# A dilated convolution on one core: start-up reordered, one-bank PSUM tiles, dummy matmuls ahead of the data

## The chip, the cores and the metric

The kernel runs on one core of one Trainium2 chip. The metric is device time in microseconds (us) of one execution; lower is better. Profiles come from single executions. The span of a profile (first to last instruction) is 1.8 us shorter than the time of the same execution (142.9 against 144.67 us for the kernel before).

Engines are named as in the profile: PE is TensorE's matmul side, PEld its weight loads, DVE is VectorE, ACT is ScalarE, POOL is GpSimd, SP is SyncE; PEq, SPq and ACTq are sequencers. L141 is line 141 of that kernel's file.

## The reference

A 3x3 convolution with dilation 2 over a batch of 16 images of 64 channels, 64x64 pixels, giving 128 channels, all float32:

```python
for kh in range(3):
    for kw in range(3):
        output[b, co] += weight[co, ci, kh, kw] * x_pad[b, ci, kh*2:kh*2+64, kw*2:kw*2+64]
```

## The kernel before

Two images share the 128 partitions (64 channels each), so each matmul uses 64 rows of the array, and the matmuls of the two images, one on each half of the rows, run together. Weights are transposed on PE with an identity; inputs arrive as float32 and are cast to float16 by DVE and ACT. A group is two tiles of 8 image rows (512 columns each); its nine taps (the nine places of the 3x3 window) accumulate in PSUM, the memory that matmuls write, and DVE and ACT evict it, that is, copy it to where it can be stored from. PSUM space for 512 float32 columns is called a bank here.

```python
# cut to the lines that the change touches
G = 2
# ...
cpool = ctx.enter_context(tc.tile_pool(name="cpsum", bufs=4, space=bass.MemoryType.PSUM))   # four tiles of two banks
# ...
nc.gpsimd.dma_start(out=w16, in_=weight.rearrange("o i h w -> o (i h w)"))   # casts in flight
wt_ps_a = cpool.tile([CO, G * NB], f32, tag="ps", name="wt_a")               # eight taps in one tile
for t, (dh, dw) in enumerate(taps):
    # ... two transposing matmuls, one per half of the partitions ...
    if t in (3, 7):
        nc.scalar.copy(out=w_sb[:, (t - 3) * CO : (t + 1) * CO], in_=wt_ps_a[...])
# ... then four input chunks per pair, of 18, 16, 16 and 14 rows, cast by DVE and ACT in turn ...
else:   # the last group of all, tile by tile, both tiles in the same ps
    for ti in range(G):
        for t in range(ntaps):
            for hb in range(2):
                conv_matmul(x3, ps, g, ti, t, hb, t == 0, t == ntaps - 1)
        # evict ps[0] half on DVE, ps[1] half on ACT, store both
```

The order of instructions on each engine is chosen by the scheduler, not by the program text.

## Time and profile before

144.34 us, median of 4 runs. The span can be cut at two events: the first convolution matmul, and the start of the last eviction, which is when the last matmul is through.

| part of the span | from | to | us |
|---|---|---|---|
| start | 0 | first convolution matmul, 11.70 | 11.7 |
| stream | 11.70 | last eviction starts, 136.93 | 125.2 |
| tail | 136.93 | end, 142.9 | 6.0 |

These are lines of the page of the kernel before: the span, the busy shares, and the rows of the 40-slice picture (each digit is the busy share of 3.6 us, in tenths).

```profile
span 142.9 us, 2675 instructions
PE 125.9 (88%) x1170; PEld 56.0 (39%) x1170; DVE 50.8 (36%) x49; ACT 50.4 (35%) x53; POOL 21.4 (15%) x49
...
PE   0029999999999999999999999999999999999730
PEclk9999999999999999999999999999999999999995
DMA  4999999999999999999999979393958667599791
```

PE is idle for most of three slices, then full. DVE and ACT have much room. DMA is full in the first half, but once the convolution runs PE never waits for it. This is the start in the timeline of the kernel before (columns: start, duration, engine, line, operation, output<-input, and in brackets the idle time before it and what ended it).

```profile
8.07 0.38 PE L86 MATMUL wt_a<-ident,w 128*64 128x128 f16 x1 [8.07 <-DMA w<-in_weight_dram]
...
9.56 0.94 ACT L122 CAST x_sb<-x 128x896 f16<-128x896 f32 x1 [2.12 <-DMA x<-in_x_dram]
10.41 0.58 ACT L89 CAST w_sb<-wt_a 128x512 f16<-128x512 f32 x1
...
11.04 0.27 PE L86 MATMUL wt_a<-ident,w 128*64 128x128 f16 x1 [2.12 <-ACT w_sb L89]
...
11.70 8.59 PE L141 MATMUL ps<-x_sb,w_sb 64*128 64x512 f16 x58
...
15.62 0.15 PEld L141 LDWEIGHTS <-w_sb 64*128 64x128 f16 x2 [0.28 <-issue]
16.05 0.15 PEld L141 LDWEIGHTS <-w_sb 64*128 64x128 f16 x2 [0.28 <-issue]
16.46 3.55 PEld L141 LDWEIGHTS <-w_sb 64*128 64x128 f16 x34 [0.27 <-issue]
```

Three things stand here. The weights arrive at 8.07 us. The first transposes are done by about 8.9, but ACT copies them only at 10.41, because its queue holds the cast of the fourth input chunk first and that chunk arrives at 9.56; PE waits 2.12 us for the copy. And from 11.70 to 16.46 us the weight loads come in pairs mostly 0.42 us apart (0.32 before the narrower matmuls of 384 columns at the image's edge), later without gaps: PE runs at half rate for 4.7 us. The PEclk row reads 9 there all the same: it takes the clock as full until the trace's first clock record (these records lie in the packed trace; `prof` shows only what is made of them). That first record, a stretch at full clock, begins at 16.44 us, just where the gaps end; so the half rate is the clock. The end of the same timeline shows one stall:

```profile
134.21 0.69 DVE L179 COPY o_sb<-ps 128x512 f32<-128x512 f32 x1 [0.72 <-PE ps L141]
...
134.95 1.96 PE L141 MATMUL ps<-x_sb,w_sb 64*128 64x512 f16 x18 [0.78 <-DVE o_sb L179]
...
136.93 0.69 DVE L179 COPY o_sb<-ps 128x512 f32<-128x512 f32 x1 [2.03 <-PE ps L141]
```

The last tile's matmuls wait 0.78 us until DVE has evicted the other half of the PSUM tile that they write. Their nine pairs then take 1.96 us, 0.22 us a pair: that is full rate.

### The profile page before, as it was taken

The numbers are of one execution on the slowest core, as the hardware profiler recorded it, in microseconds if no ns is written. First come the engines' busy times: TensorE is split into PE (matmuls) and PEld (weight loads), VectorE is DVE, ScalarE is ACT, GpSimd is POOL, SyncE is SP. The second block draws the span as 40 slices with busy tenths as digits, with TensorE's granted clock in tenths as the row PEclk, the third lists the DMA queues.
The fourth block names the chain that finished last, engine by engine and source line by source line (L and its number), as shares of the span: only waits on it lengthen the run. The fifth ranks groups of instructions, "written<-read, shape, count | busy, mean of one in ns | idle before, by whom it ended". The sixth has DMA issues, their size and how long they took to land.

```text
span 142.9 us, 2675 instructions
## 1 busy us (share of the span) xinstructions
PE 125.9 (88%) x1170; PEld 56.0 (39%) x1170; DVE 50.8 (36%) x49; ACT 50.4 (35%) x53; POOL 21.4 (15%) x49
## 2 busy tenths in 40 slices
PE   0029999999999999999999999999999999999730
PEld 0024344444444444444444444444444444444310
DVE  0213355443535352424253534433333322222510
ACT  3245374352254325241425244522222222222410
POOL 6000003020201102020202020202002020222410
PEclk9999999999999999999999999999999999999995
DMA  4999999999999999999999979393958667599791
GB/s 115 342 398 408 414 420 413 415 427 426 421 419 432 421 417 409 423 429 409 415 380 421 430 323 431 124 411 147 390 204 330 257 280 312 218 408 390 287 390 76
DMA packets 10108, 50.66 MB, mean 355 GB/s; under 512 B 1136, under 2 KB 1264, under 8 KB 6512
## 3 DMA queue, kind: packets, MB, share of 16 engines
q0 software_dynamic: 5200, 33.18, 56.2%
q1 hardware_dynamic: 4896, 17.30, 30.9%
q8 instruction: 9, 0.15, 0.4%
q14 instruction: 3, 0.02, 0.1%
HBM read 17.07 MB, written 33.55 MB: 354 GB/s over the span
## 4 chain that ended last, share of the span: by engine, by line
issue 59%; PE 18%; POOL 11%; DMA 5%; ACT 2%; SPq 1%; POOLq 1%
PE ps L141 18%; POOL out_dram L203 11%; DMA x<-in_x_dram 5%; SPq L113 1%; ACT o_sb L171 1%; ACT x_sb L122 1%; POOLq L237 0%; POOL out_dram L185 0%; ACT w_sb L89 0%; PE wt_a L87 0%; PE wt_a L86 0%; POOLq L203 0%; POOLq L185 0%
## 5 line engine op out<-in xcount | busy, mean ns | idle before, releaser
L141 PE MATMUL ps<-x_sb,w_sb 64*128 64x512 f16 (+1 forms) x1152 | 124.4, 375 | 0.8 <-DVE o_sb L179 0.8
L141 PEld LDWEIGHTS <-w_sb 64*128 64x128 f16 x1152 | 54.7, 94 | 70.2 <-issue 4.1
L170 DVE COPY o_sb<-ps 128x1024 f32<-128x1024 f32 x31 | 38.0, 1225 | 58.5 <-PE ps L141 58.5
L171 ACT COPY o_sb<-ps 128x1024 f32<-128x1024 f32 x31 | 31.4, 1013 | 65.6 <-PE ps L141 65.6
L203 POOL DMA_DIRECT2D out_dram<-o_sb x34 | 18.0, 534 | 113.3 <-ACT o_sb L171 112.8
L122 ACT CAST x_sb<-x 128x1024 f16<-128x1024 f32 (+1 forms) x16 | 15.9, 994 | 17.1 <-DMA x<-in_x_dram 10.2
L120 DVE CAST x_sb<-x 128x1152 f16<-128x1152 f32 (+1 forms) x16 | 11.6, 726 | 25.6 <-DMA x<-in_x_dram 15.4
L86 PE MATMUL wt_a<-ident,w 128*64 128x128 f16 x8 | 1.3, 322 | 10.2 <-DMA w<-in_weight_dram 8.1
L86 PEld LDWEIGHTS <-w 128*64 128x64 f16 x9 | 1.2, 207 | 8.1 <-DMA w<-in_weight_dram 8.1
L179 DVE COPY o_sb<-ps 128x512 f32<-128x512 f32 x2 | 1.4, 691 | 2.7 <-PE ps L141 2.7
L182 ACT COPY o_sb<-ps 128x512 f32<-128x512 f32 x2 | 1.2, 586 | 3.1 <-PE ps L141 3.1
L87 PEld LDWEIGHTS <-w 128*64 128x64 f16 x9 | 1.2, 207 | 2.2 <-issue 2.2
L122 ACT ACT_TABLE_LOAD x1 | 1.3, 1283 | 0.7 <-PEq L223 0.7
L185 POOL DMA_DIRECT2D out_dram<-o_sb x2 | 1.1, 547 | 2.7 <-DVE o_sb L179 2.7
L87 PE MATMUL wt_a<-ident,w 128*64 128x128 f16 x8 | 1.4, 335 | 0.0
L89 ACT CAST w_sb<-wt_a 128x512 f16<-128x512 f32 x2 | 1.2, 583 | 0.7 <-PE wt_a L87 0.7
L72 POOL DMA_DIRECT2D w<-in_weight_dram x1 | 0.7, 675 | 0.8 <-POOLq L223 0.8
L100 POOL MEMSET x_sb<- 128x128 f16 x3 | 0.7, 235 | 0.0
L101 POOL MEMSET x_sb<- 128x128 f16 x3 | 0.7, 234 | 0.0
L87 PE MATMUL wt_b<-ident,w 128*64 128x128 f16 x1 | 0.3, 323 | 0.0
L86 PE MATMUL wt_b<-ident,w 128*64 128x128 f16 x1 | 0.3, 322 | 0.0
masks.py:199 POOL TENSOR_SCALAR_AFFINE_SELECT ident<-ident 128x128 f16<-128x128 f16 x1 | 0.3, 308 | 0.0
(6 smaller groups left out, 0.9 us busy)
## 6 DMA issues: line engine op xcount, KB each, us to landing
out_dram<-o_sb POOLq DMA_DIRECT2D x28, 1024.0 KB, 8.5
x<-in_x_dram SPq DMA_DIRECT2D x16, 512.0 KB, 9.6
x<-in_x_dram SPq DMA_DIRECT2D x8, 576.0 KB, 7.2
x<-in_x_dram SPq DMA_DIRECT2D x8, 448.0 KB, 12.2
out_dram<-o_sb POOLq DMA_DIRECT2D x6, 512.0 KB, 4.5
out_dram<-o_sb SPq DMA_DIRECT2D x2, 256.0 KB, 3.1
out_dram<-o_sb POOLq DMA_DIRECT2D x2, 256.0 KB, 3.3
w<-in_weight_dram POOLq DMA_DIRECT2D x1, 144.0 KB, 6.8
```

Source lines behind the costliest of these rows:

```text
L86: nc.tensor.matmul(out=wt_ps[0:CI, c0 : c0 + CO], lhsT=w_slice, rhs=ident)
L87: nc.tensor.matmul(out=wt_ps[CI : 2 * CI, c0 : c0 + CO], lhsT=w_slice, rhs=ident)
L89: nc.scalar.copy(out=w_sb[:, (t - 3) * CO : (t + 1) * CO], in_=wt_ps_a[:, (t - 3) * CO : (t + 1) * CO],)
L113: nc.sync.dma_start(out=x32[:, lo:hi], in_=x_pair[pb, :, lo:hi])
L120: nc.vector.tensor_copy(out=x3[:, lo:hi, pad : pad + W], in_=x32[:, lo:hi, :])
L122: nc.scalar.copy(out=x3[:, lo:hi, pad : pad + W], in_=x32[:, lo:hi, :])
L141: nc.tensor.matmul(out=po, lhsT=lhsT, rhs=rhs, start=first, stop=last)
L170: nc.vector.tensor_copy(out=o_sb0[:, sl], in_=ps[0])
L171: nc.scalar.copy(out=o_sb1[:, sl], in_=ps[1])
L179: nc.vector.tensor_copy(out=o_sb0[:, e0:e1], in_=ps[0][:, ti * NB : (ti + 1) * NB])
L182: nc.scalar.copy(out=o_sb1[:, e0:e1], in_=ps[1][:, ti * NB : (ti + 1) * NB])
L203: nc.gpsimd.dma_start(out=out_img[2 * pb + bi, :, e0:e1], in_=o_sb[bi][:, e0:e1],)
```

## The change

It aims at all three places: weights earlier, copies not behind casts, clock released before the convolution, and PSUM tiles of one bank in eight buffers. The core of the diff, with lines shortened and left out:

```diff
-    chunk_rows = [(0, GR + d)]
+    chunk_rows0 = [(0, ROWS + d), (ROWS + d, CR + d)] + chunk_rows[1:]   # first pair: 10 + 8 rows
-    cpool = ... bufs=4 ...            # tiles of two banks
+    cpool = ... bufs=8 ...            # tiles of one bank
+    w32 = wpool.tile([CO, CI * KH * KW], f32, name="w32")
+    nc.scalar.dma_start(out=w32, in_=weight.rearrange("o i h w -> o (i h w)"))
-    nc.gpsimd.dma_start(out=w16, in_=weight.rearrange("o i h w -> o (i h w)"))
+    for _ in range(9):
+        nc.tensor.matmul(out=warm_ps, lhsT=warm_sb[:, :CO], rhs=warm_sb)
+    nc.vector.tensor_copy(out=w16, in_=w32)
+    ctx.enter_context(tc.manual_schedule(engines={DVE, Activation}))     # program order there
+    emit_cast(0, chunk_rows0[0][0], chunk_rows0[0][1], "v")
+    emit_cast(0, chunk_rows0[1][0], chunk_rows0[1][1], "s")
     for t, (dh, dw) in enumerate(taps):
+        wt_ps = cpool.tile([CO, NB], f32, tag="ps", name=f"wt{t}")       # one tile per tap
+        # transposes; copies by ACT and DVE in turn
+    # casts of the other three chunks only after the weight copies
-    for g in range(ngroups): ...      # two row tiles per PSUM tile, evicted as 128x1024
+    for ti in range(ntiles): ...      # one row tile per PSUM tile, evicted as 128x512
```

Stores keep their sizes, but all those of the last pair are now issued by POOL and SP side by side; before, only its last group's were.

More of the change, by code (lines that the diff above doesn't have):

```diff
@@ L39 @@
     assert H % ROWS == 0
-    G = 2
-    assert ntiles % G == 0
-    ngroups = ntiles // G
     NB = ROWS * W
-    GR = G * ROWS
-    chunk_rows = [(0, GR + d)]
-    for g in range(1, ngroups - 1):
-        chunk_rows.append((g * GR + d, (g + 1) * GR + d))
-    chunk_rows.append(((ngroups - 1) * GR + d, H))
-    nchunks = len(chunk_rows)
-    assert nchunks == ngroups
+    CR = 2 * ROWS
+    nchunks = ntiles // 2
+    chunk_rows = [(0, CR + d)]
+    for c in range(1, nchunks - 1):
+        chunk_rows.append((c * CR + d, (c + 1) * CR + d))
+    chunk_rows.append(((nchunks - 1) * CR + d, H))
+    assert nchunks == 4
+    chunk_rows0 = [(0, ROWS + d), (ROWS + d, CR + d)] + chunk_rows[1:]
     taps = [(0, 0)]
@@ L68 @@
     opool = ctx.enter_context(tc.tile_pool(name="opool", bufs=4))
-    cpool = ctx.enter_context(tc.tile_pool(name="cpsum", bufs=4, space=bass.MemoryType.PSUM))
+    cpool = ctx.enter_context(tc.tile_pool(name="cpsum", bufs=8, space=bass.MemoryType.PSUM))
+    w32 = wpool.tile([CO, CI * KH * KW], f32, name="w32")
+    nc.scalar.dma_start(out=w32, in_=weight.rearrange("o i h w -> o (i h w)"))
     w16 = wpool.tile([CO, CI * KH * KW], f16, name="w16")
-    nc.gpsimd.dma_start(out=w16, in_=weight.rearrange("o i h w -> o (i h w)"))
     ident = wpool.tile([P, P], f16, name="ident")
@@ L77 @@
     w_sb = wpool.tile([P, ntaps * CO], f16, name="w_sb")
-    wt_ps_a = cpool.tile([CO, G * NB], f32, tag="ps", name="wt_a")
-    wt_ps_b = cpool.tile([CO, G * NB], f32, tag="ps", name="wt_b")
-    for t, (dh, dw) in enumerate(taps):
-        kh = dh // d + KH // 2
-        kw = dw // d + KW // 2
-        w_slice = w16.rearrange("o (i k) -> o i k", k=KH * KW)[:, :, kh * KW + kw]
-        wt_ps, c0 = (wt_ps_a, t * CO) if t < 8 else (wt_ps_b, 0)
-        nc.tensor.matmul(out=wt_ps[0:CI, c0 : c0 + CO], lhsT=w_slice, rhs=ident)
-        nc.tensor.matmul(out=wt_ps[CI : 2 * CI, c0 : c0 + CO], lhsT=w_slice, rhs=ident)
-        if t in (3, 7):
-            nc.scalar.copy(
-                out=w_sb[:, (t - 3) * CO : (t + 1) * CO],
-                in_=wt_ps_a[:, (t - 3) * CO : (t + 1) * CO],
-            )
-        elif t == 8:
-            nc.scalar.copy(out=w_sb[:, t * CO : (t + 1) * CO], in_=wt_ps_b[:, :CO])
     x3_bufs = []
@@ L111, in emit_input_dma, with emit_cast @@
         x32_tiles[pb] = x32
-        for lo, hi in chunk_rows:
+        for lo, hi in (chunk_rows0 if pb == 0 else chunk_rows):
             nc.sync.dma_start(out=x32[:, lo:hi], in_=x_pair[pb, :, lo:hi])
-    def emit_cast(pb, ci_):
-        lo, hi = chunk_rows[ci_]
+    def emit_cast(pb, lo, hi, engine):
         x3 = x3_bufs[pb % NXB]
         x32 = x32_tiles[pb]
-        if ci_ % 2 == 0:
+        if engine == "v":
             nc.vector.tensor_copy(out=x3[:, lo:hi, pad : pad + W], in_=x32[:, lo:hi, :])
@@ L124, with conv_matmul @@
     emit_input_dma(0)
-    for ci_ in range(nchunks):
-        emit_cast(0, ci_)
-    def conv_matmul(x3, ps, g, ti, t, hb, first, last):
+    warm_sb = wpool.tile([P, NB], f16, name="warm_sb")
+    nc.vector.memset(warm_sb, 0.0)
+    warm_ps = cpool.tile([CO, NB], f32, tag="ps", name="warm_ps")
+    for _ in range(9):
+        nc.tensor.matmul(out=warm_ps, lhsT=warm_sb[:, :CO], rhs=warm_sb)
+    nc.vector.tensor_copy(out=w16, in_=w32)
+    ctx.enter_context(
+        tc.manual_schedule(engines={mybir.EngineType.DVE, mybir.EngineType.Activation})
+    )
+    emit_cast(0, chunk_rows0[0][0], chunk_rows0[0][1], "v")
+    emit_cast(0, chunk_rows0[1][0], chunk_rows0[1][1], "s")
+    for t, (dh, dw) in enumerate(taps):
+        kh = dh // d + KH // 2
+        kw = dw // d + KW // 2
+        w_slice = w16.rearrange("o (i k) -> o i k", k=KH * KW)[:, :, kh * KW + kw]
+        wt_ps = cpool.tile([CO, NB], f32, tag="ps", name=f"wt{t}")
+        nc.tensor.matmul(out=wt_ps[0:CI, 0:CO], lhsT=w_slice, rhs=ident)
+        nc.tensor.matmul(out=wt_ps[CI : 2 * CI, 0:CO], lhsT=w_slice, rhs=ident)
+        dst = w_sb[:, t * CO : (t + 1) * CO]
+        if t % 2 == 0:
+            nc.scalar.copy(out=dst, in_=wt_ps[:, 0:CO])
+        else:
+            nc.vector.tensor_copy(out=dst, in_=wt_ps[:, 0:CO])
+    emit_cast(0, chunk_rows[1][0], chunk_rows[1][1], "v")
+    emit_cast(0, chunk_rows[2][0], chunk_rows[2][1], "s")
+    emit_cast(0, chunk_rows[3][0], chunk_rows[3][1], "v")
+    def conv_matmul(x3, ps, ti, t, hb, first, last):
         dh, dw = taps[t]
-        tile_idx = g * G + ti
-        r0 = tile_idx * ROWS
+        r0 = ti * ROWS
         lo = max(r0, -dh)
@@ L139, in conv_matmul @@
         ]
-        po = ps[hb][:, ti * NB + (lo - r0) * W : ti * NB + (hi - r0) * W]
+        po = ps[hb][:, (lo - r0) * W : (hi - r0) * W]
         nc.tensor.matmul(out=po, lhsT=lhsT, rhs=rhs, start=first, stop=last)
@@ L146 @@
         o_sb1 = opool.tile([P, HW], f32, tag="osb")
-        o_sb = (o_sb0, o_sb1)
+        first_pair = pb == 0
         last_pair = pb == npairs - 1
-        flush_after = {ngroups // 2 - 1: (0, HW // 2), ngroups - 1: (HW // 2, HW)}
         if last_pair:
-            flush_after = {g: (g * G * NB, (g + 1) * G * NB) for g in range(ngroups)}
-        for g in range(ngroups):
+            flush_after = {
+                ti: ((ti - 1) * NB, (ti + 1) * NB) for ti in range(1, ntiles - 2, 2)
+            }
+            flush_after[ntiles - 2] = ((ntiles - 2) * NB, (ntiles - 1) * NB)
+            flush_after[ntiles - 1] = ((ntiles - 1) * NB, ntiles * NB)
+        else:
+            flush_after = {
+                ntiles // 2 - 1: (0, HW // 2),
+                ntiles - 1: (HW // 2, HW),
+            }
+        for ti in range(ntiles):
             ps = [
-                cpool.tile([CO, G * NB], f32, tag="ps", name=f"ps{hb}")
-                for hb in range(2)
-            ]
-            tail_group = last_pair and g == ngroups - 1
-            if not tail_group:
-                for t in range(ntaps):
-                    first = t == 0
-                    last = t == ntaps - 1
-                    for ti in range(G):
-                        for hb in range(2):
-                            conv_matmul(x3, ps, g, ti, t, hb, first, last)
-                sl = slice(g * G * NB, (g + 1) * G * NB)
+                cpool.tile([CO, NB], f32, tag="ps", name=f"ps{hb}") for hb in range(2)
+            ]
+            for t in range(ntaps):
+                for hb in range(2):
+                    conv_matmul(x3, ps, ti, t, hb, t == 0, t == ntaps - 1)
+            if pb + 1 < npairs:
+                if ti == 2:
+                    emit_input_dma(pb + 1)
+                elif ti == 4:
+                    emit_cast(pb + 1, chunk_rows[0][0], chunk_rows[0][1], "v")
+                    emit_cast(pb + 1, chunk_rows[1][0], chunk_rows[1][1], "s")
+                elif ti == 5:
+                    emit_cast(pb + 1, chunk_rows[2][0], chunk_rows[2][1], "v")
+                    emit_cast(pb + 1, chunk_rows[3][0], chunk_rows[3][1], "s")
+            sl = slice(ti * NB, (ti + 1) * NB)
+            if ti % 2 == 0:
                 nc.vector.tensor_copy(out=o_sb0[:, sl], in_=ps[0])
@@ L172 @@
             else:
-                for ti in range(G):
-                    for t in range(ntaps):
-                        for hb in range(2):
-                            conv_matmul(x3, ps, g, ti, t, hb, t == 0, t == ntaps - 1)
-                    e0 = (g * G + ti) * NB
-                    e1 = e0 + NB
-                    nc.vector.tensor_copy(
-                        out=o_sb0[:, e0:e1], in_=ps[0][:, ti * NB : (ti + 1) * NB]
-                    )
-                    nc.scalar.copy(
-                        out=o_sb1[:, e0:e1], in_=ps[1][:, ti * NB : (ti + 1) * NB]
-                    )
-                    nc.gpsimd.dma_start(out=out_img[2 * pb, :, e0:e1], in_=o_sb0[:, e0:e1])
+                nc.scalar.copy(out=o_sb0[:, sl], in_=ps[0])
+                nc.vector.tensor_copy(out=o_sb1[:, sl], in_=ps[1])
+            if ti in flush_after:
+                e0, e1 = flush_after[ti]
+                nc.gpsimd.dma_start(out=out_img[2 * pb, :, e0:e1], in_=o_sb0[:, e0:e1])
+                if last_pair:
                     nc.sync.dma_start(
@@ L188 @@
                     )
-            if pb + 1 < npairs:
-                if g == 1:
-                    emit_input_dma(pb + 1)
-                elif g == 2:
-                    emit_cast(pb + 1, 0)
-                    emit_cast(pb + 1, 1)
-                elif g == 3:
-                    emit_cast(pb + 1, 2)
-                    emit_cast(pb + 1, 3)
-            if not tail_group and g in flush_after:
-                e0, e1 = flush_after[g]
-                for bi in range(2):
+                else:
                     nc.gpsimd.dma_start(
-                        out=out_img[2 * pb + bi, :, e0:e1],
-                        in_=o_sb[bi][:, e0:e1],
+                        out=out_img[2 * pb + 1, :, e0:e1], in_=o_sb1[:, e0:e1]
                     )
```

## The prediction

> **What bounds it now.** TensorE in the middle, latency at both ends. The timeline shows the first convolution matmul at 11.70 us and the last one's evictions starting at 136.93 us of a 142.9 us span. Between them PE is busy without a break (the windows view reads 10.00 of 10 us in every middle stretch), except one 0.78 us stall at 134.2 us, where the waits view shows PE waiting for the DVE eviction of the tail group's half. VectorE and ScalarE are at 36% and 35%; DMA runs full, about 420 GB/s, in the first half, but PE never starves.
>
> So span = start (11.7) + stream (125.2) + tail (6.0). The stream holds avoidable time: weight loads of the convolution are spaced 0.42 us a pair from 11.7 to 16.4 us, then the tail's nine pairs take 1.96 us (0.22 each). About 4.7 us run at half rate, about 2.35 us lost. The Trainium skill, "TensorE: Matmul & The Clock Gate", Part 1, says the array starts at half clock and is released after a busy free-running window of about 3.4 us; this trace agrees in kind (release about 5.4 us after the dense start at 11.04). The page's PEclk row does not show it.
>
> **What the change does.**
> 1. Start. The weights land at 8.07 us now (issued at 1.25, 6.8 us to landing on the software queue, 144 KB packed), then transposes stall 2.1 us on a ScalarE copy that itself sat behind an input cast waiting for DMA. After: ScalarE's hardware queue, raw f32 (twice the destination bytes), issued about 0.75. The first input chunk of 576 KB landed 4.4 us after its issue; weights plus the new 10-row chunk are 608 KB, so I expect both at 5.0-5.5. Then the DVE cast of weights (estimate 0.43 us, from 0.69-0.76 for 1024-1152 columns), transposes (0.11 us a pair), ScalarE's 8-row cast (estimate 0.6, waiting for its chunk at about 6.0), the first weight copy (0.27), the ninth transpose waiting for a bank. Convolution starts at about 7.1 instead of 11.7: -4.6 us, all critical.
> 2. Nine dummy matmuls fill PE from about 1.1 to 5 us (0.43 each at half rate), so the clock should be released when the convolution starts: -2.35 us if so, about 0 if the burst straddles two windows. I give the release about 65%.
> 3. One-bank PSUM tiles in 8 buffers: the 0.78 us tail stall goes. Evictions are halved: DVE two of 0.69 for one of 1.23, ScalarE two of 0.59 for 1.01, some 5 us more busy time each, off the critical path.
> 4. Casts in program order: inputs are prefetched less far ahead, still about 15 us early. No PE gain or loss expected.
> 5. Matmuls and weight loads of the convolution: same number (1152); the tail after the last matmul stays about 6.0 us.
>
> **Sum.** 144.3 - 4.6 - 0.8 - (2.35 or 0) = 136.6 or 138.9; predicted 137.2 us, 8 in 10 within 135.8 to 139.8. Faster by over 2%: 0.94; within 2%: 0.05; slower: 0.01.
>
> **What would show it.** Timeline: weights' cast on DVE near 5.2-5.6, first convolution matmul near 7.1, weight loads spaced 0.21 us a pair from there (0.42 means the warm-up failed). Waits: no PE wait of note after the start; last matmul about 122 us after the first; 6.0 us after it. DMA row: less than full in the first half, fuller later.
>
> **What would make it wrong.** Weights delayed behind input packets (start at 8 or later); clock not released; ScalarE's in-order cast of the late chunk holding all weight copies; evictions held behind a cast that waits for input, stalling PE in mid-stream; output stores backing up at the end, lengthening the tail.

## The result, and the profile after

136.95 us median (136.78 to 139.25, 11 runs) against 144.44 us (143.44 to 145.03, 15 runs). The ratio is 0.949 (95% interval 0.947 to 0.952). Ratios here are the mean time of one kernel's fast runs over that of the other's fast runs of the same rounds, so they are not quite the ratio of the medians.

Ten of the 11 runs lie between 136.78 and 137.15 us. The eleventh, 139.25 us, is the one whose profile came first; the record classes it as slow, and the ratio leaves it out. So the unaltered kernel was run again (label after_again: 137.13 us median, 136.95 to 137.20, 6 runs), and its profile, of an execution of 137.12 us, is the one shown here. From its page:

```profile
span 135.2 us, 2764 instructions
PE 127.0 (94%) x1179; PEld 57.9 (43%) x1179; DVE 56.5 (42%) x87; ACT 53.7 (40%) x86; POOL 19.9 (15%) x45
...
PE   6799999999999999999999999999999999999910
PEclk9999999999999999999999999999999999999998
DMA  4999999999999999999999999999979294799790
```

Its timeline, start and end:

```profile
1.19 3.62 PE L110 MATMUL warm_ps<-warm_sb 128*128 128x512 f16 x9 [1.19 <-DVE warm_sb L107]
...
5.07 0.46 DVE L111 CAST w<-w 128x576 f16<-128x576 f32 x1 [3.93 <-DMA w<-in_weight_dram]
5.58 0.33 PE L122 MATMUL wt<-ident,w 128*64 128x128 f16 x1 [0.77 <-DVE w L111]
5.90 0.62 ACT L103 CAST x_sb<-x 128x512 f16<-128x512 f32 x1 [3.45 <-DMA x<-in_x_dram]
6.42 0.94 ACT L126 CAST w_sb<-wt 128x128 f16<-128x128 f32 x5
...
6.99 12.90 PEld L145 LDWEIGHTS <-w_sb 64*128 64x128 f16 x124
...
128.96 0.59 ACT L190 COPY o_sb<-ps 128x512 f32<-128x512 f32 x1 [1.16 <-PE ps L145]
```

Weights are in at 5.07 us, the copies follow their transposes (ACT's after its 8-row cast), the convolution starts at 7.00, its weight loads run without gaps from the first on, and the last eviction starts at 128.96. The waits view has no wait of PE for anything once the convolution has begun. From the chain of waits of the same profile (start, duration, what):

```profile
0.74 4.31 DMA w<-in_weight_dram
7.06 115.70 PE ps L145 x1093
```

Cut as above, with the profiled executions of the other runs for later use:

| profile | start | stream | tail | span |
|---|---|---|---|---|
| before | 11.70 | 125.23 | 5.97 | 142.9 |
| changed (after_again) | 7.00 | 121.96 | 6.24 | 135.2 |
| changed, the 139.25 us execution | 7.03 | 123.73 | 6.24 | 137.0 |
| no_warm | 7.21 | 123.23 | 6.26 | 136.7 |
| old_weight_load | 8.27 | 123.54 | 6.29 | 138.1 |
| unsplit_first | 7.98 | 123.65 | 6.27 | 137.9 |
| free_schedule | 9.90 | 123.91 | 6.19 | 140.0 |
| before_in_order | 10.45 | 124.46 | 5.99 | 140.9 |
| before_tail_banks | 11.58 | 123.33 | 6.89 | 141.8 |
| weights_first | 6.70 | 121.96 | 6.24 | 134.9 |
| split_tail | 6.92 | 121.99 | 6.39 | 135.3 |

So of the 7.7 us of span, the start gave 4.70, the stream 3.27, and the tail took back 0.27. Five profiles with full rate throughout have a stream of 121.96 to 121.99 us (the two not in the table are those of after_beside, 121.96, and of copies_first_split_tail, 121.98), whatever was done around it; that is the pace of PE.

The slow execution of the same kernel differs in one thing. These are its weight loads at the start:

```profile
7.02 0.13 PEld L145 LDWEIGHTS <-w_sb 64*128 64x128 f16 x4
...
9.67 0.15 PEld L145 LDWEIGHTS <-w_sb 64*128 64x128 f16 x2 [0.27 <-ACT x_sb L103]
10.09 0.15 PEld L145 LDWEIGHTS <-w_sb 64*128 64x128 f16 x2 [0.27 <-issue]
10.52 9.45 PEld L145 LDWEIGHTS <-w_sb 64*128 64x128 f16 x88 [0.27 <-issue]
```

The loads are 0.42 us apart until 10.52: 3.5 us at half rate. The dummy matmuls had run, but the clock had not been released: the trace's first clock record, at full clock, begins at 10.65 us, against 4.27 us in after_again, and the transposes before the convolution take 0.32 us here against 0.28 there. DMA is as busy in both (the slices after the first read 9), so it does not explain the half rate. Nor does only a slow run show it: no_warm below does.

### The profile page after: what moved, and what is told of

The parts are those of the page before. It is cut to its first block, busy times and chain, and to the rows that moved or that the text cites. A ratio compares the mean times of both kernels' runs of the same rounds, so it can differ in the third digit from the quotient of the medians.

```text
span 137.0 us, 2764 instructions
## 1 busy us (share of the span) xinstructions
PE 129.0 (94%) x1179; PEld 58.3 (43%) x1179; DVE 56.5 (41%) x87; ACT 54.0 (39%) x86; POOL 19.9 (14%) x45
## 2 busy tenths in 40 slices
DMA packets 10252, 50.80 MB, mean 371 GB/s; under 512 B 1152, under 2 KB 1152, under 8 KB 6656
## 4 chain that ended last, share of the span: by engine, by line
PE 87%; issue 4%; DMA 3%; POOL 1%; POOLq 0%; DVE 0%
PE ps L145 86%; DMA w<-in_weight_dram 3%; PE wt L122 1%; POOL out_dram L195 1%; POOLq L234 0%; DVE w L111 0%; PE wt L123 0%; POOLq L195 0%
## 5 line engine op out<-in xcount | busy, mean ns | idle before, releaser
L145 PEld LDWEIGHTS <-w_sb 64*128 64x128 f16 x1152 | 56.0, 94 | 67.5 <-issue 1.9
L191 DVE COPY o_sb<-ps 128x512 f32<-128x512 f32 x32 | 22.1, 692 | 35.3 <-PE ps L145 35.3
L187 DVE COPY o_sb<-ps 128x512 f32<-128x512 f32 x32 | 22.1, 692 | 33.0 <-PE ps L145 33.0
L188 ACT COPY o_sb<-ps 128x512 f32<-128x512 f32 x32 | 18.8, 587 | 36.8 <-PE ps L145 36.8
L190 ACT COPY o_sb<-ps 128x512 f32<-128x512 f32 x32 | 18.8, 587 | 35.1 <-PE ps L145 35.1
L103 ACT CAST x_sb<-x 128x1024 f16<-128x1024 f32 (+2 forms) x16 | 15.6, 977 | 4.3 <-DMA x<-in_x_dram 4.3
L101 DVE CAST x_sb<-x 128x1024 f16<-128x1024 f32 (+3 forms) x17 | 11.8, 696 | 1.5 <-DMA x<-in_x_dram 1.5
L110 PE MATMUL warm_ps<-warm_sb 128*128 128x512 f16 x9 | 4.0, 631 | 1.2 <-DVE warm_sb L107 1.2
L110 PEld LDWEIGHTS <-warm_sb 128*128 128x128 f16 x9 | 1.2, 141 | 3.1 <-issue 1.9
L122 PE MATMUL wt<-ident,w 128*64 128x128 f16 x9 | 1.3, 328 | 0.6 <-DVE w L111 0.6
L123 PE MATMUL wt<-ident,w 128*64 128x128 f16 x9 | 1.3, 329 | 0.0
L126 ACT CAST w_sb<-wt 128x128 f16<-128x128 f32 x5 | 1.1, 266 | 0.0
L128 DVE CAST w_sb<-wt 128x128 f16<-128x128 f32 x4 | 1.0, 292 | 0.2 <-PE wt L123 0.2
```

What stands on the lines that cost most here:

```text
L101: nc.vector.tensor_copy(out=x3[:, lo:hi, pad : pad + W], in_=x32[:, lo:hi, :])
L103: nc.scalar.copy(out=x3[:, lo:hi, pad : pad + W], in_=x32[:, lo:hi, :])
L110: nc.tensor.matmul(out=warm_ps, lhsT=warm_sb[:, :CO], rhs=warm_sb)
L122: nc.tensor.matmul(out=wt_ps[0:CI, 0:CO], lhsT=w_slice, rhs=ident)
L123: nc.tensor.matmul(out=wt_ps[CI : 2 * CI, 0:CO], lhsT=w_slice, rhs=ident)
L145: nc.tensor.matmul(out=po, lhsT=lhsT, rhs=rhs, start=first, stop=last)
```

## The experiments

All outputs are right. Each set was run beside the kernel before on the same chip; "before" is given where a ratio is used.

### after_again and no_warm: what the dummy matmuls are worth

after_again is the changed kernel, unedited.

> The changed kernel, unaltered, to catch a profile of its common state and to count how often it is in the other. Theory (clock luck): the profile seen so far was the one of 11 executions at 139.25 us, in which the array was still at half rate for the first 3.5 us of the convolution; a profile near 136.95 us starts the convolution at the same 7.0 us but with weight loads spaced 0.21 us a pair, so that the stream is about 121.9 to 122 us instead of 123.75. Rival (chip state): the stream is longer throughout or DMA is slower, the start of the stream looks the same.

Measured: as above, 137.13 us, six runs of six near 137. The stream is 121.96 us against 123.73 in the slow execution, and the difference lies in its first 3.5 us. The theory held; the rival (slower throughout) fell.

no_warm takes the dummies away:

```diff
-    warm_sb = wpool.tile([P, NB], f16, name="warm_sb")
-    nc.vector.memset(warm_sb, 0.0)
-    warm_ps = cpool.tile([CO, NB], f32, tag="ps", name="warm_ps")
-    for _ in range(9):
+    for _ in range(0):
```

> The changed kernel without its nine dummy matmuls. Theory: the convolution still starts at about 7.0 us, at half rate[...]; loss 1.7 to 3 us, so about 138.7 to 140 us, near the 139.25 us outlier. Rival (dummies do nothing, the release depends on the convolution alone): 137 us, as before.

Measured: 138.46 us median (138.16 to 139.06, 6 runs), ratio to before 0.961 (0.956 to 0.965) against 0.950 for after_again on the same chip. Start 7.21, stream 123.23. So dummies do matter, but by about 1.3 us, less than the 1.7 to 3 expected:

```profile
9.43 0.15 PEld L142 LDWEIGHTS <-w_sb 64*128 64x128 f16 x2 [0.27 <-issue]
9.84 10.24 PEld L142 LDWEIGHTS <-w_sb 64*128 64x128 f16 x96 [0.26 <-ACT x_sb L103]
```

Here the half rate ends at 9.84 (clock record 9.81), 2.6 us after the convolution began, and not 4.7 as in the profile before. The dense work had begun with the transposes at 5.74.

### old_weight_load: the weights' path

```diff
-    w32 = wpool.tile([CO, CI * KH * KW], f32, name="w32")
-    nc.scalar.dma_start(out=w32, in_=weight.rearrange("o i h w -> o (i h w)"))
+    nc.gpsimd.dma_start(out=w16, in_=weight.rearrange("o i h w -> o (i h w)"))
-    nc.vector.tensor_copy(out=w16, in_=w32)
```

> The changed kernel, but weights again by the software queue of GpSimd with the cast in flight. Theory: weights land at about 7.5 to 8.1 us instead of 5.25, so the convolution starts at 9.0 to 9.8 instead of 7.03: 2 to 2.8 us longer, about 139.2 us if the clock stays released over the 2.5 us pause after the dummies, up to 141.5 if not. Rival (the weight path matters little, the gain of the start lies in the order of casts and copies): within 0.7 us of the changed kernel.

Measured: 139.82 us median (139.42 to 140.04, 4 runs). The transposes started at 7.03 and the convolution at 8.27, earlier than the 9.0 to 9.8 expected: the load landed 5.7 us after its issue, not 6.8 as in the kernel before. The path itself is worth 1.27 us of start (8.27 less 7.00). The rest of the loss, 1.6 us, is in the stream. The windows view shows it (columns: stretch, PE, PEld, DVE, ACT, POOL busy with counts, then the granted clock, DMA share, GB/s):

```profile
6.00:7.00 1.00, 0.00 (x0) 0.00 (x0) 0.00 (x0) 0.00 (x0) 0.00 (x0) 1.00 1.01 393
7.00:8.00 1.00, 0.97 (x16) 0.97 (x18) 0.48 (x3) 0.60 (x3) 0.00 (x0) 1.00 1.01 413
8.00:9.00 1.00, 1.00 (x12) 0.44 (x12) 1.00 (x4) 0.98 (x4) 0.00 (x0) 0.54 1.06 431
9.00:10.00 1.00, 1.00 (x8) 0.45 (x6) 0.43 (x2) 0.62 (x1) 0.00 (x0) 0.50 1.03 403
```

The dummies had released the clock, PE then sat idle for 2.0 us (the dummies' last matmul ended at 5.01, the transposes began at 7.03), and the clock fell back to half just before the convolution began, for 3.4 us (the clock records read full from 4.67, half from 8.09, full from 11.50). Weights that came late lost twice here.

### free_schedule and before_in_order: the order on ACT and DVE

free_schedule gives the order in the changed kernel back to the scheduler:

```diff
-    ctx.enter_context(
-        tc.manual_schedule(engines={mybir.EngineType.DVE, mybir.EngineType.Activation})
-    )
```

> The changed kernel with the automatic order on VectorE and ScalarE given back. As built, ScalarE's cast of the 16-row chunk 2 and VectorE's cast of chunk 1 now stand ahead of the weight copies. Theory (most of the earlier start comes from weight copies no longer queuing behind a cast that waits for input): that chunk landed at 8.4 us and its cast takes 1.05, so the weight copies start near 9.5 and the convolution near 9.8 us instead of 7.0: 2.7 us more, plus up to 1.7 for a clock that goes back over the pause; 139.7 to 141.3 us. Rival (the fixed order matters for the steady stream, or not at all): start unchanged at 7.0 us, within 0.5 us of 137.1.

Measured: 141.98 us median (141.38 to 142.87, 4 runs), ratio to before 0.983. The weights landed as early as ever, but:

```profile
5.22 0.46 DVE L111 CAST w<-w 128x576 f16<-128x576 f32 x1 [4.09 <-DMA w<-in_weight_dram]
...
8.33 1.05 ACT L103 CAST x_sb<-x 128x1024 f16<-128x1024 f32 x1 [1.92 <-DMA x<-in_x_dram]
9.28 0.99 ACT L123 CAST w_sb<-wt 128x128 f16<-128x128 f32 x5
...
9.59 0.27 PE L119 MATMUL wt<-ident,w 128*64 128x128 f16 x1 [2.66 <-ACT w_sb L123]
```

The weight copies stand behind a cast that waits for its chunk until 8.33, and the ninth transpose waits 2.66 us for the bank that the first copy frees. The convolution starts at 9.90, 2.9 us late, and at half rate again (stream 123.91). In this execution the dummies had not released the clock at all: its first clock record is at 13.86 us, and the transposes before take 0.32 us. This is the pattern of the kernel before, brought back by one line. The time came out above the expected 139.7 to 141.3, because start and clock both lost as much as was allowed for, and a little more (2.90 us against 2.7, and 1.95 of stream against 1.7).

before_in_order is the opposite: the kernel before plus that line only.

```diff
     w_sb = wpool.tile([P, ntaps * CO], f16, name="w_sb")
+    ctx.enter_context(
+        tc.manual_schedule(engines={mybir.EngineType.DVE, mybir.EngineType.Activation})
+    )
```

> The kernel before with only the fixed program order on VectorE and ScalarE, nothing else. Theory: weights still land at about 8.05 us, the copies follow the transposes at once, the convolution starts at about 9.5 to 9.9 instead of 11.6: about 142.1 us against 143.9, ratio 0.985 to 0.99. Rival (the 2 us stall at the start is due to the PSUM tile shared by eight taps, not to the order): start unchanged, ratio 1.00.

Measured: 143.13 us (142.76 to 143.43, 4 runs) against 144.44; ratio 0.991 (0.987 to 0.994). The start moved from 11.70 to 10.45, in the expected direction but less than expected:

```profile
8.38 0.38 PE L89 MATMUL wt_a<-ident,w 128*64 128x128 f16 x1 [8.38 <-DMA w<-in_weight_dram]
...
9.14 0.58 ACT L92 CAST w_sb<-wt_a 128x512 f16<-128x512 f32 x1 [7.13 <-PE wt_a L90]
9.78 0.27 PE L89 MATMUL wt_a<-ident,w 128*64 128x128 f16 x1 [0.56 <-ACT w_sb L92]
```

ACT now copies at once, but the weights were 0.3 us later in this execution, and PE still waits 0.56 us, because the second four taps write the same PSUM tile that ACT is reading. So the rival was partly right: order explains most of the stall (1.56 of 2.12 us). The rest is put down to the shared tile by the releaser that the trace names; no run gave it separate tiles.

### unsplit_first: the split first input chunk

```diff
-    chunk_rows0 = [(0, ROWS + d), (ROWS + d, CR + d)] + chunk_rows[1:]
+    chunk_rows0 = chunk_rows
-    emit_cast(0, chunk_rows0[1][0], chunk_rows0[1][1], "s")
```

> The changed kernel with the first input chunk whole again (18 rows). Theory: the split is worth little: the chunk lands at about 6.0, its cast takes 0.76 on VectorE ahead of the weight copies there, so the second tap's weights are late by some 0.5 us, the convolution starts at 7.2 to 7.6: 137.3 to 137.8 us. Rival (the input, not the weights, sets the start): 138 us or more.

Measured: 139.66 us median (139.47 to 139.71, 4 runs). The expectation of 137.3 to 137.8 missed, and not for the reason that the rival gave. The start was 7.98, and what moved it were the weights:

```profile
6.27 0.46 DVE L111 CAST w<-w 128x576 f16<-128x576 f32 x1 [5.14 <-DMA w<-in_weight_dram]
...
7.98 6.32 PE L144 MATMUL ps<-x_sb,w_sb 64*128 64x512 f16 x42
```

The weights landed at 6.27 instead of 5.07, although neither their queue nor their size had changed. In the trace's records of single transfers, the 128 weight rows of 2304 bytes run from 1.94 to 5.72 us, side by side with 128 input rows of 4608 bytes (1.74 to 5.64). In after_again the same rows run from 2.08 to 4.61, side by side with input rows of 2560 bytes (1.75 to 4.43). So the two loads ran side by side throughout, and the weights landed later beside the longer rows. That the engines alternate between the queues row by row would explain it, but the records do not name the engine, so it is not shown. PE's pause after the dummies then grew to 1.58 us and the clock fell back in this profile too (0.50 from 9 to 12 us in the windows view, stream 123.65).

### before_tail_banks: the stall at the end

The kernel before, with PSUM tiles of its own for the very last row tile:

```diff
                 for ti in range(G):
+                    if ti > 0:
+                        ps = [cpool.tile([CO, G * NB], f32, tag="ps", name=f"psl{hb}") for hb in range(2)]
                     for t in range(ntaps):
```

> The kernel before, with one thing changed: the second half of its last group gets PSUM tiles of its own, so that it need not wait for the eviction of the first half. Theory: the 0.78 us stall of PE before the last 18 matmuls goes and nothing else: 143.6 us against 144.4, ratio about 0.995. Rival (the stall only moves the last matmuls relative to stores that end at the same time): no change.

Measured: 143.57 us (143.21 to 144.72, 6 runs) against 143.92; ratio 0.996 (0.992 to 1.001), so no difference is shown. The stall itself is gone, and the tail grew from 5.97 to 6.89 us:

```profile
132.93 1.94 PE L141 MATMUL psl<-x_sb,w_sb 64*128 64x512 f16 x18
...
134.91 0.69 DVE L184 COPY o_sb<-psl 128x512 f32<-128x512 f32 x1 [1.09 <-PE psl L141]
```

The windows view has the DMA engines at 0.91 to 1.06 of their time from 134 to 139 us, at 361 to 422 GB/s. The stores of the last 2 MB were the limit there, so matmuls that finish earlier wait for stores. This execution also had a shorter stretch at half rate (2.65 us against 4.7), so it is better compared with before_in_order, which keeps the stall and whose last eviction starts at the same 134.91 us: there the tail is 5.99 us, 0.90 less. In this pair the stores took back all of the 0.78 us, as the rival said; one pair of executions does not say how much is left on average.

### weights_first, copies_first, split_tail: a faster one?

weights_first issues the weights on SP's queue ahead of the inputs, and moves ACT's 8-row cast behind the weight copies:

```diff
-    nc.scalar.dma_start(out=w32, in_=weight.rearrange("o i h w -> o (i h w)"))
+    nc.sync.dma_start(out=w32, in_=weight.rearrange("o i h w -> o (i h w)"))
     emit_cast(0, chunk_rows0[0][0], chunk_rows0[0][1], "v")
-    emit_cast(0, chunk_rows0[1][0], chunk_rows0[1][1], "s")
     # ... transposes and weight copies ...
+    emit_cast(0, chunk_rows0[1][0], chunk_rows0[1][1], "s")
```

> An attempt at a faster one: weights are issued first on the queue of SyncE, ahead of the input chunks, so they do not share the first packets with them; the 8-row cast moves behind the weight copies on ScalarE. Theory (the start is the chain weights landing, cast, transposes, copies): weights land at about 4.2 to 4.6 instead of 5.05 to 5.25, convolution at 6.2 to 6.5 instead of 7.0, 136.3 to 136.6 us, ratio to the changed kernel 0.995. Rival (input chunk becomes the last to arrive): convolution starts at 7.0 or later, no gain.

Measured: 136.52 us median (136.14 to 137.33, 6 runs), ratio to before 0.945 (0.942 to 0.949). The weights were in at 3.51 us, even earlier than expected, which fits the reading of unsplit_first. The start moved only to 6.70, because other things took over:

```profile
3.51 0.46 DVE L111 CAST w<-w 128x576 f16<-128x576 f32 x1 [2.37 <-DMA w<-in_weight_dram]
...
5.00 0.33 PE L121 MATMUL wt<-ident,w 128*64 128x128 f16 x1
...
5.69 0.49 DVE L101 CAST x_sb<-x 128x640 f16<-128x640 f32 x1 [1.72 <-DMA x<-in_x_dram]
6.10 0.88 DVE L127 CAST w_sb<-wt 128x128 f16<-128x128 f32 x4
```

The dummies held PE until 5.00, and DVE's copies stood behind a cast whose input was now the later one. Five of its six times lie below all 29 of the kernels with the changed kernel's start. It was run at another time. Its interval overlaps that of after_beside, so the gain of some 0.4% is likely rather than shown.

copies_first tried to collect the rest: DVE's weight copies ahead of its first input cast, and seven dummies instead of nine.

> Weights first on SyncE's queue, and now also: VectorE's weight copies ahead of its first input cast, ScalarE's 8-row cast after the weight copies, seven dummy matmuls instead of nine so that the transposes may start as soon as the weights are cast. Theory: transposes from about 4.2 us, copies done by 5.7, and the first input cast (its chunk landed at 5.7, 0.49 to cast) becomes the last step: convolution at 6.2 instead of 6.7 (weights first) and 7.0 (changed kernel); 135.9 to 136.3 us. Rival (fewer dummies cost the clock): 137 to 138 us, weight loads spaced 0.42 us at the start.

Measured: 137.45 us median, in two clusters: 136.27, 136.29, 136.73 and 138.17, 138.29, 138.32. The profile fell in the slower one and shows PE waiting 1.5 us for the input cast, start 7.08, then half rate until 9.71. The input chunk came at 6.44 instead of 5.69. By their times, half of the runs show the rival, fewer dummies costing the clock. In the profile the transposes, right after the dummies, already take 0.32 us and not 0.28, so the clock had not been released when PE's pause before the convolution began; whether it would have been without that pause was not separated.

split_tail is the changed kernel with the very last row tile computed, evicted and stored in two halves of four rows each.

> The changed kernel with its very last tile computed, evicted and stored in two halves of four rows. Theory (the end is eviction plus a store of 512 KB after the last matmul): half the eviction (about 0.4 us instead of 0.69) and half the last store: 0.4 to 0.8 us less, 136.2 to 136.6 us. Rival (the end is set by the store bandwidth of the last 2 MB, as in the kernel before with its tail stall removed, or by fixed time after the last store): within 0.2 us of the changed kernel.

Measured: 137.04 us median (136.88 to 138.70, 6 runs) beside after_beside at 137.01: no gain. The last evictions started at 128.91 and DVE's took 0.42 instead of 0.69 us, yet the tail was 6.39. The windows view says why:

```profile
129.00:130.00 1.00, 0.00 (x0) 0.00 (x0) 0.37 (x1) 0.28 (x1) 0.72 (x2) 1.00 1.00 391
130.00:131.00 1.00, 0.00 (x0) 0.00 (x0) 0.00 (x0) 0.00 (x0) 0.12 (x1) 1.00 1.00 391
131.00:132.00 1.00, 0.00 (x0) 0.00 (x0) 0.00 (x0) 0.00 (x0) 0.00 (x0) 0.76 1.03 389
132.00:133.00 1.00, 0.00 (x0) 0.00 (x0) 0.00 (x0) 0.00 (x0) 0.00 (x0) 0.50 0.07 25
```

DMA is full until 132 us; the tail is store bandwidth and some 3 us in which nothing moves. The rival was right.

copies_first_split_tail has both edits of these two.

> Both of the above together. Theory (start and end add up): 135.2 to 135.9 us, ratio to the changed kernel about 0.99. Rival: no more than the better of the two alone.

Measured: 136.72 us median (136.36 to 138.33), again two runs of six at 138.2 and above. No more than the better of its parts. Its profile, of 136.87 us, is at full rate (clock record 4.52) and still starts at 6.82, because PE waits 1.27 us for the first input cast: with the weights ahead of them, the inputs set the start.

after_beside was the yardstick:

> The changed kernel once more, as the yardstick on the same chip for the three that follow: 136.9 to 137.2 us, with one execution in ten or so near 139 us.

Measured: 137.01 us median (136.94 to 138.16, 6 runs). Over all runs with nine dummies and the changed kernel's start (after, after_again, after_beside, split_tail), 26 of 29 lie between 136.78 and 137.20, and three at 138.16 to 139.25. With seven dummies it is five of twelve at 138.17 to 138.33.

## Why the prediction was right or wrong

It said 137.2 us (135.8 to 139.8), and 136.95 was measured. Point by point:

1. **Start, -4.6 us predicted, -4.70 measured: right.** Weights were expected at 5.0 to 5.5 (5.07), the convolution at 7.1 (7.00). The prediction used the Trainium skill's "TensorE: Matmul & The Clock Gate" only for the clock; the start came from durations in the trace. What it left open is the split among the causes. In one profile each, undone one by one in the changed kernel, the order on ACT and DVE cost 2.9 us of start, the old weight path 1.27, the unsplit chunk 0.98. These sum to 5.15, more than the whole of 4.7, so they overlap. The order is the largest there; added alone to the kernel before it gave 1.25. Not undone on their own were the weight copies tap by tap on both engines, the one-bank tiles in the main loop and the last pair's stores on two engines. The prediction named the queue behind the input cast, but its item on program order spoke of prefetch alone. That the split of the input chunk helps through the weights' landing was not foreseen.
2. **Clock, "-2.35 us if so, about 0 if the burst straddles two windows", at 65%: right in mechanism, mis-sized twice.** Judged by their times, the release worked in 26 of 29 runs, not in 65%. Between the two profiles the stream lost 3.27 us: the stall of 0.78, and 2.49 of half rate, close to 2.35. But the dummies account for only 1.27 us of it (the streams of no_warm and after_again; 1.33 in the medians, 138.46 less 137.13). The other 1.2 us came mostly because the half rate lasted 4.7 us in the one profile of the kernel before that the forecast was read from, and only 2.6 us in no_warm. The stretch varies: 2.8 us in before_tail_banks and 3.2 in before_in_order, by the clock records. That the whole of 2.35 seemed to come true is luck of that profile. The missed state was predicted at 138.9 us; the three misses are 138.16, 138.70 and 139.25.
3. **"The 0.78 us tail stall goes": it went, but the 0.8 us in the sum was too much.** The stream lost the stall, and the tail grew from 5.97 to 6.24 us in the changed kernel. In the kernel before, with last evictions at the same 134.91 us, the tail is 6.89 us without the stall (before_tail_banks) and 5.99 with it (before_in_order). The tail "stays about 6.0 us" was therefore slightly wrong: it is bound by stores, as one of the listed risks said.
4. **Program order of casts, no effect in mid-stream: right.** No PE wait after the start, stream 121.96 us against "about 122". Input loads did end later: the last is issued at 82.2 us after the change, against 63.9 before. It lands at 95.5, 18 us ahead of the last pair's first matmul at 113.5.
5. **"DMA row: less than full in the first half, fuller later": half wrong.** It is fuller later (full up to slice 29 instead of 23), but the first half stayed full (399 GB/s on average over the first 20 slices in both).
6. **Matmuls unchanged: right**, 1152 of them in both, median 375 ns.

The sum for a released clock was 136.6, and 136.95 was measured. Its savings were read from an execution of 144.67 us but taken off the median of 144.3; taken off 144.67 they give 136.92, and the profiled execution of the changed kernel took 137.12. Between these two profiles start, stream and tail changed by -4.70, -3.27 and +0.27 us, against -4.6, -3.15 and 0 in the forecast. The stated 137.2 lies between two states, 136.6 and 138.9, so that it is only 0.25 us off is partly luck too. The kernel before spreads from 143.4 to 145.3 over the sets. That this follows from the varying half-rate stretch is likely but not shown: only one execution of it was profiled.

## What to carry to other kernels

Look at what stands ahead of the first instructions on the critical chain: one cast that waited for a late chunk held all weight copies on ACT here, and giving up the fixed order cost more start than giving up the faster load path (2.9 against 1.27 us). A load that the start waits for can lose to large neighbours on other queues: the weights landed in 2.7 us when issued first on the inputs' queue, and in 4.3 or 5.5 us beside inputs. Dummy matmuls seem to have brought nothing where PE then paused for 1.6 to 2.0 us before the transposes (streams of 123.65 and 123.54 us, against 123.23 in no_warm); pauses of 0.8 and 1.3 us did no harm in the profiles of after_again and copies_first_split_tail. Before shortening a tail, see whether the stores are already at full bandwidth there.

## What the Trainium skill lacked or had wrong

- "TensorE: Matmul & The Clock Gate", Part 1, says that the clock is released after a busy window of about 3.4 us and that the window runs freely. It calls the window busy, or sustained, but does not say how full it must be. In after_again the clock record shows the release 3.1 us after the first dummy (1.19 to 4.27 us), so the window was not full; in after_beside, weights_first and split_tail it came 3.5, 3.6 and 4.0 us after. By the times, nine dummies of 3.6 to 4.0 us were enough in 26 of 29 runs.
- The same page, "Why this matters for your kernels", warns of PE idle gaps longer than about 3 us. Here a gap of 2.02 us (old_weight_load) and one of 1.58 us (unsplit_first), each with 1.2 us of small transposes between it and the convolution, were followed by a fall to half clock for 3.4 us. If the transposes did not count as work, the gaps would be 3.26 and 2.77 us; no run tells the two readings apart.
- No page that was read says that the profile's clock row omits the half rate before the first release: in the kernel before it reads 9 (full) up to 16.4 us, where the first clock record stands, while weight loads are 0.42 us a pair. It does show a later fall (0.54 and 0.50 in old_weight_load).
- "DMA: Bandwidth & Descriptors", "Queues, rings and completion order", says that an engine drains a packet of some 9 to 17 descriptors from one queue before it turns to the next. It does not say what a load loses beside another queue's. Here two loads of 128 rows each ran side by side all along (which engine carried which row is not recorded), and the weights landed 2.7, 4.3 or 5.5 us after their issue, as they went first on the inputs' own queue, beside rows of 2560 bytes, or beside rows of 4608 bytes.
- "Trainium Kernel Development and Optimization", "Key Constraints", says that DMAs from all queues interleave on the same 16 engines, so that a second queue saves issue time only. The runs do not contradict this, and add that a load sharing the engines from a queue of its own can land later (4.3 us) than as the first on a shared one (2.7 us).
